# Row maxima and inverse sums of two attention mixers, turned by TensorE or by VectorE

## The chip, the cores and the metric

The kernel runs on one core of a Trainium2 chip. The metric is the device time of one execution in microseconds (us), as the median of several runs. A core has TensorE (PE, matmuls; its weight loads are shown as PEld), VectorE (DVE), ScalarE (ACT), GpSimd (POOL) and SyncE (SP), which here only issues DMAs. Each engine works off its own instructions in order; engines wait for each other at semaphores. SBUF is the working memory with 128 partitions; TensorE writes to PSUM, which has eight banks per partition.

## The reference

One step of a hybrid diffusion layer: 128 context tokens (the prompt) and 1024 latent tokens, width 1024. Each token tile is normalised, modulated and projected to queries, keys, values and gates of two attention mixers, with 8 query heads on 2 key heads each. Mixer A attends over all latent keys and 128 cached ones; mixer B over a band of 128 on each side plus the cached keys, with a learned sink in the softmax:

```python
s = jnp.einsum('bqkgd,bskd->bkgqs', qblk, k_all).astype(jnp.float32) * (d ** -0.5)
p = jax.nn.softmax(s, axis=-1).astype(v_all.dtype)
...
s = jnp.concatenate([sink_column(sink, kv, s_ctx.shape[:-1]), s_ctx, s_band], axis=-1)
p = jax.nn.softmax(s, axis=-1).astype(v_lat.dtype)
...
return jnp.concatenate([o_a * jax.nn.silu(g_a), o_b * jax.nn.silu(g_b)], axis=-1) @ w_out
```

All arrays are float32. The kernel keeps that precision by splitting operands into a high part in fp32r and a low remainder, with two or three products for each.

## The kernel before

The first 280 us hold the modulation, the projections and the gates. The rest is the attention, in units: a unit is one tile of 128 queries (t), one mixer (m = 0 for A, 1 for B) and one group of four heads (g). Units alternate, A then B, so that a pair is one A and one B unit of the same tile and group; there are 16 pairs of latent tiles, and two for the prompt (t = 0). A loop over slots, one slot for one block of 128 keys of one unit, issues all instructions: in each slot first what the agenda holds (`later(n, f)` puts f on it n slots ahead), then the scores of this slot's block, then work that is due there for later units, then products of the output projection, and the value products of the block three slots before. `in_order` at the end keeps each engine's instructions in this order.

**Mixer A.** `max_items` runs ahead of the unit. It takes twelve products `pmx` (L998) of queries and keys, and DVE reduces each to row maxima (L999). `finish` fetches the low part of the queries into the tile qb (L1003, issued by SP) and reduces the twelve maxima of each row to four, one per head, in `m_nat` (L1007): queries lie on the partitions, heads in the columns. The maxima are needed the other way round: as four more rows (64 to 67) of qb, which has queries along its free axis, so that the product of qb with the low keys (L1334) subtracts the maximum as well. `transpose` is put on the agenda by `TURN`. It turns m_nat by a product with the identity into a PSUM bank (`ptm`, L1012), and DVE multiplies the turned rows with `diag`, minus the identity of four, into qb (L1013, one instruction of 4 x 512). The scores `st` (L1333, L1334) then go through ACT's exponential (L1336) and its rounding to the high part (L1340); POOL subtracts for the low part (L1344). `st` lies in the two banks of tag B, so that the scores of one block wait for the exponential two blocks before. Tag A, also two banks, holds `pmx`, `ptm` and part of mixer B's scores.

**Mixer B.** `weight_items` runs ahead of its unit. For each head it makes scores `sn` (L1086, L1087), adds the mask and takes the row maximum on DVE (L1090), and takes the exponential on ACT (L1056) with the row sums. For t > 1 ("boxed") DVE turns the weights in 32 x 32 squares in place (L1066), and DMAs out and back (L1071, L1076) finish the turn. When the unit's slots come, ACT rounds the weights to the high part (L1318) and the low part is subtracted on POOL for even blocks (L1322) and on DVE for odd ones (L1320). The weights aren't divided by their sums; the gate is. `divide` takes the reciprocal of the sums (L1124, again queries on partitions, heads in four columns). `turned` turns it by a product with the identity (`pti`, L1136, tag B for boxed tiles), `put` copies it to SBUF (L1140) and writes it to the DRAM scratch `r_dram` with one DMA (L1141), `rows` fetches it back, spread over 64 partitions for each head (L1146), and POOL multiplies the unit's gate with it (L1132). `ROWS_AT` are their places behind `divide`.

The small tiles m_nat and diag lie in the pool `few`; diag is made on POOL at the start (L372), from the identity.

Of the kernel before, what the change touches and what calls it, by code (L numbers as in the profile page):

```python
# [9 lines left out]
F32 = mybir.dt.float32  # L10
F32R = mybir.dt.float32r
BF16 = mybir.dt.bfloat16
AF = mybir.ActivationFunctionType
ALU = mybir.AluOpType
AX = mybir.AxisListType
# [3 lines left out]
P = 128  # L19
# [20 lines left out]
EARLY = (0, 2)  # L40
# [31 lines left out]
QTS = 5  # L72
PROMPT_LEAD = 4
EX_AT = (2, 2, 5)
ROWS_AT = (1, 1, 4, 6)
BOX_BACK = 2
PROMPT_KEYS_AT = 12
KV_ORDER = [0] + list(range(1, NT))
# [39 lines left out]
def hybrid_step(ctx, tc, x_prompt, x_sample, cache_k_a, cache_v_a, cache_k_b, cache_v_b,  # L118
# [3 lines left out]
    nc = tc.nc  # L122
# [10 lines left out]
    r_dram = [dram.tile([4, P], F32, name=f"rd{i}") for i in range(2 * NL)]  # L133
# [4 lines left out]
    def later(n, f):  # L138

        agenda.setdefault(now[0] + n, []).append(f)  # L140
# [13 lines left out]
    def bank(tag, name):  # L154
        return ps.tile([P, 512], F32, tag=tag, name=name, bufs=BANKS[tag])
# [11 lines left out]
    ident_r = cst.tile([P, P], F32R, name="ident_r")  # L167
# [3 lines left out]
    few = ctx.enter_context(tc.tile_pool(name="few", bufs=1, side="right"))  # L171
# [2 lines left out]
    mhalf = few.tile([P, 8], F32, name="mhalf")  # L174
    nc.vector.memset(mhalf, -0.5)

    m_nat = [few.tile([P, 4], F32R, name=f"m_nat{i}") for i in range(2)]
    diag = few.tile([4, 4], F32, name="diag")
    few.tile([P, 8], F32, name="pad0")

    def rsqrt_mean(pool, ss, n, width, name):

# [150 lines left out]
    with tc.tile_pool(name="st", bufs=2, side="right") as st:  # L333
        ident = st.tile([P, P], F32, name="ident", bufs=1)
# [32 lines left out]
        def conditions():  # L367

            nc.scalar.copy(colt, pcol)
            nc.gpsimd.tensor_scalar(bsc1, colt[:, 32:40], 1.0, None, op0=ALU.add)  # L370
            nc.gpsimd.tensor_copy(ident_r, ident)
            nc.gpsimd.tensor_scalar(diag, ident[0:4, 0:4], -1.0, None, op0=ALU.mult)  # L372

        def modulate_rows(j, half=2):
            if half != 1:
# [136 lines left out]
        for t in (1, 2, 3, 4):  # L512
            squares(t)
            if t == 2:
                nc.scalar.activation(silc, pcol[:, 0:16], AF.Silu)
        conditions()
        for t in (5, 6):
            padded(t, nc.gpsimd)
# [34 lines left out]
        for j in range(1, KT + 3):  # L553
# [68 lines left out]
            if KT - 2 <= j < KT:  # L622
# [3 lines left out]
                c0, n = W_QA.cols[0]  # L626
# [51 lines left out]
    with tc.tile_pool(name="qt", bufs=2, side="right") as qt:  # L678
# [85 lines left out]
        for m in range(2):  # L764
            w, nxt = ((W_QA, W_QB), (W_QB, W_KV))[m]
            ts = list(range(1, NT)) + [0]
            for t in ts:
# [3 lines left out]
                if (m, t) in ((0, ts[-2]), (1, ts[GATE_AT[0]])):  # L771
                    n = len(wg) // 2
# [95 lines left out]
    with ktp:  # L868
# [74 lines left out]
        for n, t in enumerate(KV_ORDER):  # L943
            if n < AHEAD:
                tick()
                pk, v = pks[n]
# [21 lines left out]
    qtile, qbtile, mxtile, sgl = {}, {}, {}, {}  # L968
# [12 lines left out]
    def max_items(i):  # L981

        t, m, g = units[i]
        out = []

        def item(h, b):
            if h == 0 and b == 0:
                mxtile[i] = qs.tile([P, 4, 3], F32, tag="mx", name=f"mx{i}", bufs=3)
            mx = mxtile[i]
            lhs = qtile[i][:, P * h : P * h + P]  # L990
            pm = bank("B" if i == APART + 1 else "A", f"pmx{i}_{h}_{b}")
            if t == 0:
                for h in range(4):
                    hs = slice(P * h, P * h + P)
                    nc.tensor.matmul(pm[:, hs], qtile[i][:, hs], khb[:, g, 0, :], start=True, stop=True)
                nc.vector.tensor_reduce(mx[:, :, 0], pm.rearrange("p (h n) -> p h n", h=4), axis=AX.X, op=ALU.max)
            else:
                nc.tensor.matmul(pm[:, 0:384], lhs, kha[:, g, 3 * b : 3 * b + 3, :], start=True, stop=True)  # L998
                nc.vector.tensor_reduce(mx[:, h, b : b + 1], pm[:, 0:384], axis=AX.X, op=ALU.max)  # L999

        def finish():
            qb_ = qp.tile([68, 512], F32R, tag="qb", name=f"qb{i}", bufs=2)
            nc.sync.dma_start(qb_[0:64, :].bitcast(F32), q_dram[t][m][0:64, 512 * g : 512 * g + 512])  # L1003
            qbtile[i] = qb_
            mx = mxtile.pop(i)
            mn = m_nat[i // 2 % 2]
            nc.vector.tensor_reduce(mn, mx if t else mx[:, :, 0:1], axis=AX.X, op=ALU.max)  # L1007
            later(TURN[boxed(t)], transpose)

        def transpose():  # L1010
            pt = bank("E" if i in EARLY else "A", f"ptm{i}")
            nc.tensor.transpose(pt[0:4, 0:P].bitcast(F32R), m_nat[i // 2 % 2], ident_r)  # L1012
            nc.vector.tensor_tensor(qbtile[i][64:68, :].rearrange("p (h n) -> p h n", h=4),  # L1013
                                    pt[0:4, 0:P].unsqueeze(1).to_broadcast([4, 4, P]),
                                    diag.unsqueeze(2).to_broadcast([4, 4, P]), op=ALU.mult)

        for h in range(4 if t else 1):
            for b in range(3 if t > 0 else 1):
                out.append(lambda h=h, b=b: item(h, b))
        return out, finish  # L1020

    def boxed(t):

        return t > 1
# [5 lines left out]
    def weight_items(i):  # L1030

        t, m, g = units[i]
        v = {}
# [73 lines left out]
        def finish():  # L1107
            (nc.gpsimd if t else nc.vector).tensor_tensor(v["ex"], v["nm"], sink[:, 4 * g : 4 * g + 4], op=ALU.add)
            if t:
                for n, f in zip(EX_AT if i > 3 else EX_EARLY, (sinks, total, divide)):  # L1110
                    later(n, f)
            else:
                sinks()
                later(1, total)
                later(1, divide)
# [5 lines left out]
            (nc.gpsimd if t else nc.vector).tensor_tensor(v["sum"], v["sum"], v["ex"], op=ALU.add)  # L1121

        def divide():
            nc.vector.reciprocal(v["inv"], v["sum"])  # L1124
            if t == 0:
                nc.vector.tensor_tensor(penat[i], penat[i], v["inv"].unsqueeze(2).to_broadcast([P, 4, P]), op=ALU.mult)
                return

            later(ROWS_AT[0], turned)
            later(ROWS_AT[1], put)  # L1130
            later(ROWS_AT[2], rows)
            later(ROWS_AT[3], lambda: nc.gpsimd.tensor_tensor(sgl[i], sgl[i], v["rows"], op=ALU.mult))  # L1132

        def turned():
            v["pt"] = bank("B" if boxed(t) else "A", f"pti{i}")[0:4, 0:P]
            nc.tensor.transpose(v["pt"], v["inv"], ident_r.bitcast(F32))  # L1136

        def put():
            iv = spare[0:4, 512 : 512 + P]
            (nc.vector.tensor_copy if i < 2 or boxed(t) else nc.scalar.copy)(iv, v["pt"])  # L1140
            nc.sync.dma_start(r_dram[i // 2], iv)  # L1141

        def rows():
            v["rows"] = spare[:, 512:768].rearrange("p (c n) -> p c n", c=2)
# [83 lines left out]
    for f in beside[2]:  # L1228
# [5 lines left out]
        name=nc.get_next_instruction_name(), engine=mybir.EngineType.Activation, act_func_set_id=6))  # L1234
# [5 lines left out]
    spare, gate = None, []  # L1240
# [232 lines left out]
    for i, (t, m, g) in enumerate(units):  # L1473
        if i in EARLY:
            continue
        if m == 0:
            items, done = max_items(i)
            at = [start[i - 2] + a for a in (MX_EARLY if i == 4 else MX_AT)]
            end = start[i] - MX_LEAD
            if t == 0:  # L1480
                end = start[i] - LEAD - g
                at = [end - 1]
        else:
            items, done = weight_items(i)
            at = [start[i - 1] + j for j in (NAT_AT if i > 3 else NAT_EARLY)] if t else [start[i] - PROMPT_LEAD]
            end = at[-1] + 1
        if i >= LOADED:
            first = max(start[i - QTS + 1] - 1, at[0] - LOADLEAD[m], 0)
            assert first < at[0] or first == 0, (i, first, at)
            put(first, lambda i=i: u_load(i))  # L1490
        for s, f in zip(at, items):
            put(s, f)
        put(end, done)
# [103 lines left out]
```

## Time and profile before

| what | time |
|---|---|
| median of 3 runs | 682.07 us (681.73 to 682.82) |
| the profiled execution | 683.28 us |
| span of its trace | 681.3 us |
| granted TensorE clock in the span | 0.999 |
| attention, from 300 to 660 us: PE busy | 356.77 of 360 us |
| DVE busy there | 279.35 us |
| ACT busy there | 291.74 us |
| POOL busy there | 271.20 us |

The profile is that of one execution. Its page gives the busy time of each engine, the chain of work that ended last, and the groups of instructions by line: engine, operation, tiles out<-in with their shapes, count, busy time, mean duration in ns, and the idle time of the engine just before them with what ended it. A timeline lists instructions by start time with their duration; "x2" merges neighbours of one group, and brackets tell how long the engine idled before and for what. Matmuls are pipelined: the next one starts before the end shown for the last.

### The profile page before, as it was taken

What the parts mean: (1) busy time and instruction counts of PE and PEld (TensorE: products, weight loads), DVE (VectorE), ACT (ScalarE), POOL (GpSimd) and SP (SyncE); (2) the same over time, 40 slices, a digit from 0 to 9 for tenths busy, and PEclk for the clock granted to TensorE, in tenths of its full rate; (3) what the DMA queues carried; (4) which work ended last, traced back from release to release, by engine and by line L of the source; (5) the groups of instructions that cost most, each with busy time, mean ns of one, the idle gap of its engine ahead of it and who ended that gap; (6) DMA issues with size and microseconds to landing.
All of it is one profiled execution on the core that took longest, in us unless ns stands there. A gap on an engine that the chain in (4) does not pass through costs nothing.

```text
span 681.3 us, 10630 instructions
## 1 busy us (share of the span) xinstructions
PE 671.4 (99%) x3325; PEld 535.6 (79%) x3325; DVE 491.9 (72%) x1055; ACT 403.8 (59%) x834; POOL 373.4 (55%) x378
## 2 busy tenths in 40 slices
PE   8999999999999999999999999999999999999997
PEld 4678988878788888997767777877777777777766
DVE  4776257877787872856788888788787887886663
ACT  6666412411233243169778877877798779878770
POOL 3556024233222250248687669766876787678861
PEclk9999999999999999999999999999999999999999
DMA  8971283349445024541275445664555455544524
GB/s 350 405 266 64 79 314 78 82 91 298 117 117 150 16 90 150 178 140 60 86 201 177 146 151 173 186 191 134 170 178 165 147 161 170 194 124 155 180 68 124
DMA packets 75852, 107.74 MB, mean 158 GB/s; under 512 B 9297, under 2 KB 43533, under 8 KB 75797
## 3 DMA queue, kind: packets, MB, share of 16 engines
q1 hardware_dynamic: 67556, 95.11, 43.6%
q10 hardware_dynamic: 8240, 11.96, 6.5%
q8 instruction: 26, 0.43, 0.2%
q14 instruction: 30, 0.24, 0.1%
HBM read 73.24 MB, written 33.80 MB: 157 GB/s over the span
## 4 chain that ended last, share of the span: by engine, by line
PE 92%; DVE 2%; ACT 2%; DMA 2%; issue 1%; POOL 0%; SPq 0%; ACTq 0%; DVEq 0%
PE po L1434 13%; PE pv L1357 6%; PE pv L1354 6%; PE pmx L998 5%; PE pq L270 5%; PE pq L268 5%; PE pq L269 5%; PE st L1334 5%; PE st L1333 5%; PE pv L1356 5%; PE pg L282 3%; PE pg L278 3%; PE pg L283 3%; PE pk L269 2%; PE pk L270 2%; PE pk L268 2%
## 5 line engine op out<-in xcount | busy, mean ns | idle before, releaser
L1344 POOL TENSOR_TENSOR pl<-pe,ph 128x512 fp32r<-128x512 f32 x128 | 165.8, 1301 | 71.8 <-ACT ph L1340 49.7
L999 DVE TENSOR_REDUCE mx<-pmx 128x1 f32<-128x384 f32 x192 | 100.1, 547 | 28.9 <-PE pmx L998 28.6
L1336 ACT ACTIVATE pe<-st 128x512 f32<-128x512 f32 x146 | 86.6, 593 | 13.3 <-PE st L1334 12.4
L1340 ACT CAST ph<-pe 128x512 fp32r<-128x512 f32 x146 | 90.7, 621 | 5.6
L1354 PE MATMUL pv<-ph,v_hi 128*128 128x512 f32 x208 | 82.2, 395 | 0.2 <-ACT pen L1056 0.2
L1357 PE MATMUL pv<-pl,v_hi 128*128 128x512 f32 x208 | 82.2, 395 | 0.2 <-DVE pl L1330 0.2
L186 POOL TENSOR_TENSOR rs_q<-ms_q,mhalf 128x8 f32<-128x8 f32 x18 | 34.2, 1899 | 80.8 <-DVE ms_q L184 80.8
L1434 PE MATMUL po<-wo,ogh 128*128 128x512 f32 (+1 forms) x224 | 73.3, 387 | 0.0
L1056 ACT ACTIVATE pen<-sn,nm 128x512 f32<-128x512 f32 (+2 forms) x72 | 45.0, 626 | 37.0 <-DVE nm L1090 33.5
L1090 DVE CUSTOM_DVE_ANT_0 sn<-sn,mask,nsink 128x512 f32<-128x512 f32 (+1 forms) x64 | 45.9, 717 | 19.4 <-PE sn L1087 12.5
L998 PE MATMUL pmx<-kha,qt 128*128 128x384 f32 x192 | 58.5, 351 | 0.8 <-DVE mx L999 0.7
L1334 PE MATMUL st<-qb,kla 68*128 68x512 f32 x144 | 57.5, 399 | 0.7 <-DVE qb L1013 0.4
L1333 PE MATMUL st<-qt,kha 128*128 128x512 f32 x144 | 57.8, 401 | 0.0
L1356 PE MATMUL pv<-ph,v_lo 128*64 128x512 f32 x146 | 57.7, 395 | 0.0
L1357 PEld LDWEIGHTS pv<-pl,v_hi 128*128 128x128 f32 x208 | 39.1, 188 | 17.5 <-DVE pl L1330 0.6
L998 PEld LDWEIGHTS pmx<-kha,qt 128*128 128x128 f32 x192 | 36.3, 189 | 13.9 <-DVE mx L999 3.6
L1354 PEld LDWEIGHTS pv<-ph,v_hi 128*128 128x128 f32 x208 | 39.1, 188 | 8.5 <-ACT pen L1056 0.6
L1434 PEld LDWEIGHTS po<-wo,ogh 128*128 128x128 f32 x224 | 41.0, 188 | 5.7 <-ACT ogh L1396 0.3
L747 ACT CAST qo0q<-ptq 128x512 fp32r<-128x512 f32 x18 | 10.6, 587 | 57.8 <-PE ptq L744 57.8
L1434 PE MATMUL po<-wo,ogl 128*128 128x512 f32 (+1 forms) x112 | 43.5, 388 | 0.0
L1322 POOL TENSOR_TENSOR pl<-pen,ph 128x512 fp32r<-128x512 f32 x28 | 37.2, 1328 | 8.1 <-ACT ph L1318 8.1
L1066 DVE STREAM_TRANSPOSE pen<-pen 128x512 f32<-128x512 f32 (+1 forms) x56 | 37.0, 677 | 5.6 <-ACT pen L1056 5.4
(258 smaller groups left out, 1720.5 us busy)
## 6 DMA issues: line engine op xcount, KB each, us to landing
td<-pen SPq DMA_DIRECT2D x24, 512.0 KB
pen<-td SPq DMA_DIRECT2D x96, 128.0 KB
qt<-qd SPq DMA_DIRECT2D x36, 256.0 KB
wm<-in_w_mod_ss_dram SPq DMA_DIRECT2D x7, 1024.0 KB
qd<-qo0q ACTq DMA_DIRECT2D x36, 128.0 KB
qd<-qo1q ACTq DMA_DIRECT2D x36, 128.0 KB
sgl<-gd SPq DMA_DIRECT2D x35, 128.0 KB
out_dram<-yt SPq DMA_DIRECT2D x17, 256.0 KB
```

The costliest lines, as they stand in the source:

```text
L268: nc.tensor.matmul(out, h_at(0, i, k, tok), w.hi[k], start=(k == 0), stop=False)
L998: nc.tensor.matmul(pm[:, 0:384], lhs, kha[:, g, 3 * b : 3 * b + 3, :], start=True, stop=True)
L999: nc.vector.tensor_reduce(mx[:, h, b : b + 1], pm[:, 0:384], axis=AX.X, op=ALU.max)
L1333: nc.tensor.matmul(s, kh, qtile[i], start=True, stop=False)
L1334: nc.tensor.matmul(s, kl, qbtile[i], start=False, stop=True)
L1336: nc.scalar.activation(pe, s, AF.Exp)
L1340: nc.scalar.copy(ph, pe)
L1344: nc.gpsimd.tensor_tensor(pl, pe, ph, op=ALU.subtract)
L1354: nc.tensor.matmul(pv, two, ph, start=(b == 0), stop=False)
L1356: nc.tensor.matmul(pv[0:64, :], vl, ph, start=False, stop=False)
L1357: nc.tensor.matmul(pv, two, pl, start=False, stop=last)
L1434: nc.tensor.matmul(po[n, q.start], a, wo_parts[KT * n + k][lo][:, q], start=(k == KS[0] and p == 0), stop=(k == KS[-1] and p == 2))
```

## The change

m_nat becomes 32 columns wide. Where PE turned it, DVE now turns it in place, in four squares of 32 x 32: the maxima of queries a to a+31 then lie on partitions a to a+3, for a = 0, 32, 64 and 96. Four DVE products of 4 x 128 with a diag that is repeated at those partitions write qb's four rows, 32 queries at a time. In mixer B the reciprocal goes straight into the first four columns of a new tile, `turned_inv`, which DVE turns the same way in the same slot; `put` has no copy left, and writes four DMAs of 4 x 32 numbers in place of one. PE's products `ptm` and `pti` and their banks go. The three tiles are filled with zeros by POOL at the start. The entries of `ROWS_AT` that stay keep their places.

```diff
-ROWS_AT = (1, 1, 4, 6)
+ROWS_AT = (1, 4, 6)
...
-    m_nat = [few.tile([P, 4], F32R, name=f"m_nat{i}") for i in range(2)]
-    diag = few.tile([4, 4], F32, name="diag")
-    few.tile([P, 8], F32, name="pad0")
+    m_nat = [few.tile([P, 32], F32R, name=f"m_nat{i}") for i in range(2)]
+    turned_inv = few.tile([P, 32], F32, name="turned_inv")
+    diag = few.tile([P, 4], F32, name="diag")
+    for a in m_nat + [turned_inv]:
+        nc.gpsimd.memset(a.bitcast(F32), 0.0)
...
-            nc.gpsimd.tensor_scalar(diag, ident[0:4, 0:4], -1.0, None, op0=ALU.mult)
+            for a in range(0, P, 32):
+                nc.gpsimd.tensor_scalar(diag[a : a + 4], ident[a : a + 4, a : a + 4], -1.0, None, op0=ALU.mult)
...
-            nc.vector.tensor_reduce(mn, mx if t else mx[:, :, 0:1], axis=AX.X, op=ALU.max)
+            nc.vector.tensor_reduce(mn[:, 0:4], mx if t else mx[:, :, 0:1], axis=AX.X, op=ALU.max)
             later(TURN[boxed(t)], transpose)
...
         def transpose():
-            pt = bank("E" if i in EARLY else "A", f"ptm{i}")
-            nc.tensor.transpose(pt[0:4, 0:P].bitcast(F32R), m_nat[i // 2 % 2], ident_r)
-            nc.vector.tensor_tensor(qbtile[i][64:68, :].rearrange("p (h n) -> p h n", h=4),
-                                    pt[0:4, 0:P].unsqueeze(1).to_broadcast([4, 4, P]),
-                                    diag.unsqueeze(2).to_broadcast([4, 4, P]), op=ALU.mult)
+            mn = m_nat[i // 2 % 2].bitcast(F32)
+            nc.vector.transpose(mn, mn)
+            for a in range(0, P, 32):
+                nc.vector.tensor_tensor(qbtile[i][64:68, :].rearrange("p (h n) -> p h n", h=4)[:, :, a : a + 32],
+                                        mn[a : a + 4].unsqueeze(1).to_broadcast([4, 4, 32]),
+                                        diag[a : a + 4].unsqueeze(2).to_broadcast([4, 4, 32]), op=ALU.mult)
...
-            nc.vector.reciprocal(v["inv"], v["sum"])
+            nc.vector.reciprocal(turned_inv[:, 0:4] if t else v["inv"], v["sum"])
...
-            later(ROWS_AT[0], turned)
-            later(ROWS_AT[1], put)
-            later(ROWS_AT[2], rows)
-            later(ROWS_AT[3], lambda: nc.gpsimd.tensor_tensor(sgl[i], sgl[i], v["rows"], op=ALU.mult))
-
-        def turned():
-            v["pt"] = bank("B" if boxed(t) else "A", f"pti{i}")[0:4, 0:P]
-            nc.tensor.transpose(v["pt"], v["inv"], ident_r.bitcast(F32))
+            nc.vector.transpose(turned_inv, turned_inv)
+            later(ROWS_AT[0], put)
+            later(ROWS_AT[1], rows)
+            later(ROWS_AT[2], lambda: nc.gpsimd.tensor_tensor(sgl[i], sgl[i], v["rows"], op=ALU.mult))
...
         def put():
-            iv = spare[0:4, 512 : 512 + P]
-            (nc.vector.tensor_copy if i < 2 or boxed(t) else nc.scalar.copy)(iv, v["pt"])
-            nc.sync.dma_start(r_dram[i // 2], iv)
+            for a in range(0, P, 32):
+                nc.sync.dma_start(r_dram[i // 2][:, a : a + 32], turned_inv[a : a + 4])
```

## The prediction

> **What bounds the kernel now.** I read the page first: busy time by engine, then the chain that ended last.
>
> ```profile
> PE 671.4 (99%) x3325; PEld 535.6 (79%) x3325; DVE 491.9 (72%) x1055; ACT 403.8 (59%) x834; POOL 373.4 (55%) x378
> ...
> PE 92%; DVE 2%; ACT 2%; DMA 2%; issue 1%; POOL 0%; SPq 0%; ACTq 0%; DVEq 0%
> ```
>
> TensorE is busy 99% of the span and holds 92% of the chain, so work taken off it looks like time won. But matmul ends are modelled and overlap, so a busy PE can hide short stalls. I therefore went on to the groups by line with shapes kept apart, for what goes and what resembles what comes:
>
> ```profile
> L999 DVE TENSOR_REDUCE mx<-pmx 128x1 f32<-128x384 f32 x192 | 100.1, 547 | 28.9 <-PE pmx L998 28.6
> ...
> L1066 DVE STREAM_TRANSPOSE pen<-pen 128x512 f32<-128x512 f32 x48 | 32.5, 695 | 4.4 <-ACT pen L1056 4.3
> ...
> L1382 DVE TENSOR_TENSOR spare<-pv,rs 64x256 f32<-64x256 f32 x64 | 26.4, 413 | 0.5
> ...
> L1136 PE MATMUL pti<-ident_r,inv 128*4 128x128 f32 x16 | 4.4, 273 | 0.0
> ...
> L1013 DVE TENSOR_TENSOR qb<-ptm,diag 4x512 fp32r<-4x512 f32 x18 | 12.3, 682 | 0.6
> ...
> L1140 DVE COPY spare<-pti 4x128 f32<-4x128 f32 x15 | 4.1, 273 | 0.0
> L1012 PE MATMUL ptm<-ident_r,m_nat 128*4 128x128 f32 x18 | 4.0, 222 | 0.0
> ...
> L1124 DVE RECIPROCAL inv<-sum 128x4 f32<-128x4 f32 x18 | 3.0, 169 | 0.1
> ```
>
> Then the timeline of the attention, one pair of units at a time (some 22.4 us each). First, what one small product really costs PE, by starts:
>
> ```profile
> 354.12 0.40 PE L1357 MATMUL pv<-pl,v_hi 128*128 128x512 f32 x1
> ...
> 354.35 0.22 PE L1012 MATMUL ptm<-ident_r,m_nat 128*4 128x128 f32 x1
> ...
> 354.42 0.44 PE L1086 MATMUL sn<-khb,qt 128*128 128x512 f32 x1
> ...
> 354.70 0.40 PE L1087 MATMUL sn<-klb,qt 128*128 128x512 f32 x1
> ```
>
> A 512-column product hands over after 0.23 us. ptm hands over after 0.07, and the product behind it takes 0.28 instead of 0.23: ptm costs PE 0.12 us, not its 222 ns. I take pti alike. All 34 are worth 34 x 0.12 = 4.1 us if PE never waits.
>
> Second, what PE waits for at the start of a mixer A unit. This is the pair around 402 us:
>
> ```profile
> 400.68 1.30 POOL L1322 TENSOR_TENSOR pl<-pen,ph 128x512 fp32r<-128x512 f32 x1
> ...
> 400.70 1.82 DVE L1320 TENSOR_TENSOR pl<-pen,ph 128x512 fp32r<-128x512 f32 x1
> ...
> 402.24 1.44 POOL L1322 TENSOR_TENSOR pl<-pen,ph 128x512 fp32r<-128x512 f32 x1 [0.26 <-ACT ph L1318]
> ...
> 402.55 0.68 DVE L1013 TENSOR_TENSOR qb<-ptm,diag 4x512 fp32r<-4x512 f32 x1
> ...
> 403.16 0.74 DVE L1090 CUSTOM_DVE_ANT_0 sn<-sn,mask,nsink 128x512 f32<-128x512 f32 x1
> ...
> 404.04 0.69 ACT L1056 ACTIVATE pen<-sn,nm 128x512 f32<-128x512 f32 x1 [1.88 <-DVE nm L1090]
> ...
> 406.50 0.60 ACT L1336 ACTIVATE pe<-st 128x512 f32<-128x512 f32 x1
> ...
> 407.16 0.49 PE L1333 MATMUL st<-qt,kha 128*128 128x512 f32 x1
> ```
>
> This is a chain through DVE and ACT that ends on PE. DVE makes qb (402.55 to 403.23), then adds the mask and takes the row maximum (L1090). ACT has stood idle 1.88 us for that; it runs L1056 and three more instructions without a gap, then L1336, which ends at 407.10 and so frees the bank into which PE writes its next scores at 407.16. **In this pair PE has no slack behind qb: qb later by x is PE later by x.** Around 380 us there is some:
>
> ```profile
> 379.91 1.29 POOL L1322 TENSOR_TENSOR pl<-pen,ph 128x512 fp32r<-128x512 f32 x1 [0.53 <-ACT ph L1318]
> 379.96 0.68 DVE L1013 TENSOR_TENSOR qb<-ptm,diag 4x512 fp32r<-4x512 f32 x1
> ...
> 383.39 0.69 DVE L1320 TENSOR_TENSOR pl<-pen,ph 128x512 fp32r<-128x512 f32 x1 [0.30 <-ACT ph L1318]
> ...
> 383.92 0.60 ACT L1336 ACTIVATE pe<-st 128x512 f32<-128x512 f32 x1
> ...
> 384.99 0.39 PE L1333 MATMUL st<-qt,kha 128*128 128x512 f32 x1
> ```
>
> Here L1336 ends at 384.52 and PE comes at 384.99; less 0.06 for the hand-over, 0.41 us is slack. The same order stands before twelve mixer A units, alternating between these two kinds; the first and the last of the twelve (in the first, the score product L1334 itself waits for qb):
>
> ```profile
> 357.50 0.68 DVE L1013 TENSOR_TENSOR qb<-ptm,diag 4x512 fp32r<-4x512 f32 x1
> ...
> 604.52 0.68 DVE L1013 TENSOR_TENSOR qb<-ptm,diag 4x512 fp32r<-4x512 f32 x1
> ```
>
> Third, the two L1320 above: the same instruction takes 0.69 us alone and 1.82 beside POOL's L1322. It ends 0.54 after POOL does (401.98 to 402.52). L1320 reads both inputs from SBUF. L1013, with one input in PSUM, runs through L1322 in 682 ns every time. So a DVE instruction with two SBUF inputs waits until POOL's subtraction ends. Size doesn't matter:
>
> ```profile
> 644.73 1.28 POOL L1322 TENSOR_TENSOR pl<-pen,ph 128x512 fp32r<-128x512 f32 x1
> ...
> 645.03 1.00 DVE L1103 SCALAR_TENSOR_TENSOR nm<-mx,nsink 128x4 f32<-128x4 f32 x1
> ...
> 652.86 0.16 DVE L1103 SCALAR_TENSOR_TENSOR nm<-mx,nsink 128x4 f32<-128x4 f32 x1
> ```
>
> Four columns take 1.00 us under L1322 and 0.16 without.
>
> **The change, part by part.**
>
> *Removed from PE:* 18 ptm and 16 pti, 0.12 us each. Twelve of each lie in the twelve pairs, between the POOL work that starts the chain and the scores at its end. There PE comes no sooner to the end, so these 24 win nothing. The other ten win 10 x 0.12 = 1.2 us.
>
> *Mixer A on DVE:* qb was one product of 512 columns from PSUM. It becomes a turn of 128x32 and four products of 128 columns, and m_nat and diag now both lie in SBUF. No turn of that size is in the trace: it lies between 169 ns (L1124, four columns) and 695 (L1066, sixteen times as wide); I take 0.2, near the first. It reads one tile and L1066 shows no long cases, so it isn't blocked. The products are:
>
> ```profile
> L664 DVE TENSOR_TENSOR rb_k<-knk,ksin x16: 279/285/486, 207.5 to 252.0; 128x128 f32<-128x128 f32 x16
> ```
> ```profile
> 362.67 0.84 DVE L1382 TENSOR_TENSOR spare<-pv,rs 64x256 f32<-64x256 f32 x2
> ...
> 375.37 0.99 DVE L999 TENSOR_REDUCE mx<-pmx 128x1 f32<-128x384 f32 x2
> ```
>
> One takes 0.285. Two L999 (547 ns each, above) take 0.99 together, so neighbours overlap by some 0.08 to 0.1; the two halves of L1382 (413 each), on other partitions, take 0.84, so they don't overlap. The new products read other partitions each time: 0.30 apart; the other end is 0.20.
>
> Now the order in time. L1320 ends, the turn runs 0.2 us, and meanwhile POOL's next L1322, whose input is there, has begun. The first product waits for its end. By L1320's rows 0.15 of an instruction's own time passes under the wait (0.69 less 0.54), so 0.14 of the 0.285 is left. Then come three more, 0.90. At 402: 403.68 + 1.04 = 404.72 instead of 403.23, **1.49 later**. At 380: 381.20 + 1.04 = 382.24 instead of 380.64, 1.60 later, 1.19 after the slack. L1090 stands behind qb on DVE, L1056 waits for it, PE for L1336, as above. With seven of the first kind and five of the second: 7 x 1.49 + 5 x 1.19 = **16.4 us**. If PE came late only where ACT does, and everything else moves with it, nothing gives it back: PE is the bound for the rest of the pair.
>
> By the Trainium skill, "VectorE: DVE Perf Modes", section "Two Vector instructions with no wait between them", an instruction whose input starts in another group of 32 partitions than the last one's is held until all earlier ones end. The four products would each be held, which fits L1382's row; without it the spacing would be 0.20 and the sum 12 x 0.3 = 3.6 us less.
>
> *Mixer B on DVE:* the turn (0.2) comes in right behind the reciprocal, and the copy (0.27), a little later, goes. Around 375 us the L999 shown last stands directly behind the reciprocal, and PE waits for it:
>
> ```profile
> 375.95 0.44 PE L998 MATMUL pmx<-kha,qt 128*128 128x384 f32 x1
> ```
>
> There L998 comes 0.2 later, but this is PE time ahead of the chain's end, which hides it. Uncovered it costs 5 x 0.2 = 1.0. ptm and pti also give up their places in banks A and B; the bank wait that ends on PE is the one for L1336, and that stays.
>
> *SP:* 48 more issues, 0.26 us each.
>
> ```profile
> 395.74 0.38 SPq L1305 DMA_DIRECT2D sgl<-gd  x1
> 398.87 0.26 SPq L1141 DMA_DIRECT2D rd<-spare  x1
> 399.18 0.47 SPq L1003 DMA_DIRECT2D qb<-qd  x1
> ```
>
> The queue is idle before L1141 and the turned sums are there sooner than the copy was, so the four mostly fit in. Queued behind them is the fetch for qb, issued at 399.18 and needed by the scores after 403; late by all of 3 x 0.26 = 0.78 it would still have 3 us. I take nothing; without that cover it is at most 12 x 0.78 = 9 us. *Start:* three fills and three more scalings of diag on POOL, which then idles 4.16 us; nothing:
>
> ```profile
> 15.59 1.30 POOL L468 TENSOR_TENSOR h<-hf,h 128x512 fp32r<-128x512 f32 x1 [4.16 <-DVE hf L467]
> ```
>
> Sum: 683.28 (the profiled execution) + 16.4 - 1.2 = 698.5. The median shown is 682.07, 1.2 lower: **697.3**.
>
> **The rivals.**
>
> *PE time counts, faster.* For it: the 99%. Place: the 24 products in the pairs; it decides if the first product gets its read before POOL's second L1322, or if ACT makes up the lateness before PE needs the bank. Price: -34 x 0.12 = -4.1, 678.0. Against: ACT's idle 1.88 us ahead of L1056, and no gap after it. By the Trainium skill, same page, section "Rules for kernel authors", VectorE is the fastest for a turn within 32x32; no run here shows that for this size. Chance 0.10.
>
> *No wait for POOL, the products apart as L1382's.* qb is then 0.2 - 0.08 + 0.90 + 0.285 = 1.3 after L1320, against 0.71 before: 0.6 later. 7 x 0.6 + 5 x 0.2 - 1.2 = +4, 686. For it: the new tiles have four partitions, and no blocked instruction in the trace has so few. Chance 0.20.
>
> *No wait and overlapping products.* 0.3 later, 7 x 0.3 - 1.2 = +0.9, 683.0, about no change. L664's last products speak for it, L1382 against. Chance 0.07.
>
> **How the numbers follow.** The forecast, 0.63: 690 (spacing 0.20, some lateness made up) to 703 (no slack in the second kind, 5 x 0.41 = 2.0, the turn's 1.0, and some 2 for the prompt's two units, where POOL is busy too). With the second rival the range is 685 to 703; left out are the rivals that aren't slower, 0.17. A difference of 0.2% (1.4 us) is about the least that a measurement of this kernel tells from none. Faster 0.10, same 0.07, slower 0.83.
>
> **What would show it.** Right: the first of the four qb products ends some 0.14 us after an L1322, lasting near 1 us, three follow 0.3 apart; ACT's idle time ahead of L1056 grows from 1.88 to over 3; PE waits on L1336 in every pair; POOL is unchanged. Wrong: products of 0.3 us while L1322 runs, or PE's gaps before L1333 no longer than now.

## The result and the profile after

The changed kernel takes 707.85 us (median of 4 executions, 706.47 to 709.1) where the kernel before took 681.91 beside it: 1.038 times as long, with an interval of 1.036 to 1.040. It is 25.9 us slower; forecast were 15.2 (697.3), and 703 was the end of the range. The direction was right and the size was not.

One line from the page of the kernel before, then the page of the kernel after: busy time by engine, the chain that ended last, and groups by line (busy time, mean ns, idle time before them and what ended it). Line numbers differ between the kernels: L1334 of before is L1333 of after.

```profile
L1334 PE MATMUL st<-qb,kla 68*128 68x512 f32 x144 | 57.5, 399 | 0.7 <-DVE qb L1013 0.4
```
```profile
PE 679.8 (96%) x3291; PEld 533.9 (75%) x3291; DVE 520.0 (74%) x1128; ACT 403.0 (57%) x833; POOL 375.9 (53%) x384
...
PE 69%; DVE 17%; DMA 4%; ACT 4%; issue 3%; POOL 1%; SPq 1%; ACTq 0%; DVEq 0%; POOLq 0%
...
L1333 PE MATMUL st<-qb,kla 68*128 68x512 f32 x144 | 58.7, 407 | 11.0 <-DVE qb L1017 11.0
...
L1017 DVE TENSOR_TENSOR qb<-m_nat,diag 4x128 fp32r<-4x128 f32 x72 | 42.7, 593 | 1.4
```

PE's share of the chain falls from 92% to 69% and DVE's rises from 2% to 17%. The score product with qb, which waited 0.7 us before, now waits 11 us for it. The mean of 593 ns for the new products hides two kinds; the view of one line shows them (shortest, median, longest; first and last start), and so does the group of the two turns:

```profile
L1017 DVE TENSOR_TENSOR qb<-m_nat,diag x72: 282/286/1411, 282.4 to 677.9; 4x128 fp32r<-4x128 f32 x72
```
```profile
L1015 DVE STREAM_TRANSPOSE m_nat<-m_nat 128x32 f32<-128x32 f32 x18 | 3.6, 201 | 0.0
L1133 DVE STREAM_TRANSPOSE turned_inv<-turned_inv 128x32 f32<-128x32 f32 x16 | 3.4, 212 | 0.5
```

Half of the products take 0.286 us or less, as forecast, and some take four to five times that. The turn takes 0.20, as forecast. This is the timeline at the pair which the prediction showed around 402 us, now around 407:

```profile
406.71 0.69 DVE L1319 TENSOR_TENSOR pl<-pen,ph 128x512 fp32r<-128x512 f32 x1
406.77 3.08 POOL L1321 TENSOR_TENSOR pl<-pen,ph 128x512 fp32r<-128x512 f32 x2
407.32 0.20 DVE L1015 STREAM_TRANSPOSE m_nat<-m_nat 128x32 f32<-128x32 f32 x1
...
407.55 3.04 DVE L1017 TENSOR_TENSOR qb<-m_nat,diag 4x128 fp32r<-4x128 f32 x4
...
409.42 0.39 PE L1332 MATMUL st<-qt,kha 128*128 128x512 f32 x1
...
410.62 0.76 DVE L1094 CUSTOM_DVE_ANT_0 sn<-sn,mask,nsink 128x512 f32<-128x512 f32 x1
...
410.65 0.50 PE L1333 MATMUL st<-qb,kla 68*128 68x512 f32 x1 [0.84 <-DVE qb L1017]
...
411.52 0.69 ACT L1060 ACTIVATE pen<-sn,nm 128x512 f32<-128x512 f32 x1 [3.35 <-DVE nm L1094]
```

DVE's subtraction L1319 now starts 0.06 us ahead of POOL's L1321. It gets through in 0.69, and POOL's is the one that is stretched: two of them take 3.08 back to back, where 2 x 1.3 would be their own time. The four products run into both of POOL's instructions: the first one waits for one, and before the second product starts POOL has begun the next. All four take 3.04 us, where the run with POOL's fill, below, shows 1.18. And PE stands at L1333, the product that reads qb, 1.23 us after the start of L1332 instead of 0.23 (403.50 to 403.73 before, shown below).

### The profile page after: what moved, and what is told of

Same layout as the page of the kernel before. It is cut to its first block, busy times and chain, and to the rows that moved or that the text cites. A ratio compares the mean times of both kernels' runs of the same rounds, so it can differ in the third digit from the quotient of the medians.

```text
span 707.4 us, 10649 instructions
## 1 busy us (share of the span) xinstructions
PE 679.8 (96%) x3291; PEld 533.9 (75%) x3291; DVE 520.0 (74%) x1128; ACT 403.0 (57%) x833; POOL 375.9 (53%) x384
## 4 chain that ended last, share of the span: by engine, by line
PE 69%; DVE 17%; DMA 4%; ACT 4%; issue 3%; POOL 1%; SPq 1%; ACTq 0%; DVEq 0%; POOLq 0%
PE po L1433 9%; DVE qb L1017 5%; PE st L1332 4%; PE pq L270 4%; PE pq L272 4%; PE pq L271 4%; PE st L1333 4%; PE pv L1353 3%; PE pmx L1001 3%; PE pv L1356 3%; PE pg L280 3%; PE pg L284 3%; PE pg L285 3%; PE pv L1355 2%; PE pk L271 2%
## 5 line engine op out<-in xcount | busy, mean ns | idle before, releaser
L1333 PE MATMUL st<-qb,kla 68*128 68x512 f32 x144 | 58.7, 407 | 11.0 <-DVE qb L1017 11.0
L1332 PE MATMUL st<-qt,kha 128*128 128x512 f32 x144 | 60.1, 417 | 2.0 <-DVE pl L1329 0.6
L1321 POOL TENSOR_TENSOR pl<-pen,ph 128x512 fp32r<-128x512 f32 x28 | 38.9, 1395 | 11.7 <-ACT ph L1317 10.2
L1017 DVE TENSOR_TENSOR qb<-m_nat,diag 4x128 fp32r<-4x128 f32 x72 | 42.7, 593 | 1.4
```

Of the source, the lines that this page charges most:

```text
L1332: nc.tensor.matmul(s, kh, qtile[i], start=True, stop=False)
L1333: nc.tensor.matmul(s, kl, qbtile[i], start=False, stop=True)
```

## The experiments

Theory 1: the loss is the products' wait for POOL's reads of SBUF, since both their inputs now lie there. Theory 2: it is the DVE work itself, a turn and three more products on the way to qb. Theory 3: it is mixer B's half, its turn and its four small DMAs. Times are medians; the kernel before took 682.1 to 682.3 beside all of these.

### Each half alone

Mixer A's half alone: the kernel after with

```diff
-ROWS_AT = (1, 4, 6)
+ROWS_AT = (1, 1, 4, 6)
...
-            nc.vector.transpose(turned_inv, turned_inv)
-            later(ROWS_AT[0], put)
+            later(ROWS_AT[0], turned)
+            later(ROWS_AT[1], put)
...
```

> Mixer A's half of the change alone: DVE turns the maxima and multiplies them from SBUF, mixer B's inverse is turned by PE and copied as before. Theory 1 (the loss is qb's products, which have both inputs in SBUF and wait for POOL's reads, handed on over DVE, ACT and the bank to PE): 705 to 709 us, and the first or second of the four products near 1.1 to 1.3 us in every pair. Theory 3 (mixer B's turn and its 48 more DMAs cost it): 682 to 688 us.

Measured: 707.05 us (706.38 to 707.51).

Mixer B's half alone: the kernel before, with turned_inv, its turn and its four DMAs.

> Mixer B's half of the change alone. Theory 1: 679 to 682 us, since sixteen small products of PE go, at 0.12 us each by starts, of which only those beside no wait win. Theory 3 (mixer B's turn and its DMAs cost the 26 us): 700 us or more.

Measured: 679.56 us (679.07 to 680.98), 0.997 of before, interval 0.996 to 0.998: within what theory 1 gave, and faster than both kernels.

The whole loss is mixer A's, and theory 3 falls. The 2.6 us that mixer B's half wins alone (1.3 to 2.9 by the interval) are about what the rival "PE time counts" gives for its sixteen small products, 16 x 0.12 = 1.9. In the kernel after nothing is left of them: it takes 707.0 to 707.9 with that half and 707.05 without. Where PE waits for qb in every pair, earlier PE time buys nothing.

### The same DVE work without the wait

In the kernel before, qb from four products out of PSUM, and a turn of a tile of zeros on DVE:

```diff
+            nc.vector.transpose(turned_m, turned_m)
+            for a in range(0, P, 32):
+                nc.vector.tensor_tensor(qbtile[i][64:68, :].rearrange("p (h n) -> p h n", h=4)[:, :, a : a + 32],
+                                        pt[0:4, a : a + 32].unsqueeze(1).to_broadcast([4, 4, 32]),
+                                        diag.unsqueeze(2).to_broadcast([4, 4, 32]), op=ALU.mult)
```

> The kernel before, where PE still turns the maxima, but qb comes from four products of 4x128 that read the turned maxima in PSUM, and DVE also turns a tile of zeros: all the DVE work of mixer A's half and one small product of PE more than after, but no product with two inputs in SBUF. Theory 1: the work alone moves qb later by the turn of 0.20 us and three more products at 0.2 to 0.3, near 1.0 us, of which the pairs without slack hand on most: 682 to 692 us, products 0.25 to 0.3 us long. Theory 2 (it is the DVE work itself that costs, not the wait for POOL): 700 us or more.

Measured: 681.09 us (680.48 to 682.93), 0.999 of before, interval 0.998 to 1.000. The expectation had the four products too slow: they take 0.2 us more than the one product of 0.68, since they follow 0.20 apart. 700 us, as theory 2 had it, are far off. But the run doesn't show that this work is free. From one reduction of m_nat to the next, the pairs like that at 380 us go from 22.15 to 22.44 us, and those like that at 402 us from 22.73 to 22.40. In the latter DVE's subtraction (L1323 here) now gets ahead of POOL's and takes 0.69 us, as in the kernel after, where the kernel before has up to 1.82.

```profile
399.38 3.10 POOL L1325 TENSOR_TENSOR pl<-pen,ph 128x512 fp32r<-128x512 f32 x2
399.39 0.69 DVE L1323 TENSOR_TENSOR pl<-pen,ph 128x512 fp32r<-128x512 f32 x1
```

The kernel after with the turned maxima in PSUM:

```diff
-            nc.vector.transpose(mn, mn)
+            pt = bank("E" if i in EARLY else "A", f"ptm{i}")[:, 0:32]
+            nc.vector.transpose(pt, mn)
...
-                                        mn[a : a + 4].unsqueeze(1).to_broadcast([4, 4, 32]),
+                                        pt[a : a + 4].unsqueeze(1).to_broadcast([4, 4, 32]),
```

> The kernel after, but the turned maxima are written to a PSUM bank, so that the four products have one input in SBUF and one in PSUM; the small products of PE are gone as in the kernel after. Theory 1: no product waits for POOL any more and each lasts 0.3 us: qb comes about 0.6 us later than before, which gives 680 to 690 us. Theory 2: as the kernel after, 700 us or more.

Measured: 684.94 us (684.67 to 686.32), 1.005 of before, interval 1.003 to 1.007. The products of the run with PE's turn come first, in the view of their line and, for one unit, in the timeline; then those of this run in the same two views:

```profile
L1016 DVE TENSOR_TENSOR qb<-ptm,diag x72: 271/272/283, 282.2 to 649.9; 4x128 fp32r<-4x128 f32 x72
```
```profile
400.21 0.88 DVE L1016 TENSOR_TENSOR qb<-ptm,diag 4x128 fp32r<-4x128 f32 x4
```
```profile
L1018 DVE TENSOR_TENSOR qb<-ptm,diag x72: 281/288/296, 282.5 to 653.4; 4x128 fp32r<-4x128 f32 x72
```
```profile
401.68 3.03 POOL L1322 TENSOR_TENSOR pl<-pen,ph 128x512 fp32r<-128x512 f32 x2
...
402.49 1.19 DVE L1018 TENSOR_TENSOR qb<-ptm,diag 4x128 fp32r<-4x128 f32 x4
```

With one input in PSUM none of the 72 products is long in either run, POOL's subtractions notwithstanding: in the last fence the four start 0.8 us into POOL's two, and take 1.19. The one placement of the turned maxima is worth 22 us (707.01, below, to 684.94). Theory 2 is left with the rest: 684.94 is 5.4 us above mixer B's half alone, for a turn in the way of qb and products 0.30 apart.

The timelines also part the spacings: four products that all start at partition 0 take 0.88 us, (0.88 - 0.27) / 3 = 0.20 apart; four that start at partitions 0, 32, 64 and 96 take 1.19, 0.30 apart. By the Trainium skill, "VectorE: DVE Perf Modes", section "Two Vector instructions with no wait between them", only the latter are held until the one before has ended; these runs agree.

### POOL writes but doesn't read

POOL's subtraction for mixer B's even blocks becomes a fill, in the kernel before and in the kernel after:

```diff
-                nc.gpsimd.tensor_tensor(pl4, p, ph4, op=ALU.subtract)
+                nc.gpsimd.memset(pl.bitcast(F32), 0.0)
```

> The kernel before, in which POOL fills the low part of the even blocks of mixer B's weights with zeros instead of subtracting (the low part of those blocks is left out of the result). POOL then writes but reads nothing in SBUF there. It is the base for the next run. Both theories: 679 to 683 us, since POOL is not the bound.

Measured: 678.50 us (677.89 to 678.83). It fell 3.6 us under before, a little below what both theories gave. Here DVE's subtraction of the odd blocks, which also reads two tiles of SBUF, never waits: all 26 take 0.65 to 0.69 us, also where one starts 0.29 us behind the start of POOL's fills. In the kernel before, such a place took 1.57 us (378.36).

```profile
376.59 0.99 POOL L1322 MEMSET pl<- 128x512 f32 x2
376.88 0.69 DVE L1320 TENSOR_TENSOR pl<-pen,ph 128x512 fp32r<-128x512 f32 x1
```

> The kernel after with the same fill on POOL (the low part of those blocks is left out of the result). Theory 1 (qb's products wait because POOL reads SBUF at that time): the products beside the fill last 0.29 us again, and the distance to the run with the fill in the kernel before falls from 26 to 3 to 8 us, with what the prompt's units lose to POOL's other subtractions on top of the 3 us that the turn into PSUM cost. Theory 2 (any work of POOL holds them): the distance stays at 20 us or more.

Measured: 681.94 us (681.75 to 684.14), 3.4 us above the run with the fill in the kernel before. By the reductions of m_nat in the two traces, none of that lies in the twelve pairs (266.5 us before, 266.4 after): 1.4 lie ahead of them and 2.2 behind, where POOL's other subtractions still run. The timeline of one unit:

```profile
400.77 0.69 DVE L1319 TENSOR_TENSOR pl<-pen,ph 128x512 fp32r<-128x512 f32 x1
400.81 0.99 POOL L1321 MEMSET pl<- 128x512 f32 x2
...
401.37 0.20 DVE L1015 STREAM_TRANSPOSE m_nat<-m_nat 128x32 f32<-128x32 f32 x1
...
401.61 1.18 DVE L1017 TENSOR_TENSOR qb<-m_nat,diag 4x128 fp32r<-4x128 f32 x4
```

The four products take 1.18 together, 0.30 apart, although all inputs are in SBUF. The fill is also shorter than the subtraction (0.53 us against 1.3), and the first product starts only 0.19 us before the fills end, so these rows alone don't part reads from busy time. The subtraction that runs through the fills in 0.69 does. By the Trainium skill, "SBUF — State Buffer", section "Who interferes with whom", a VectorE instruction with two SBUF inputs contends with a GpSimd instruction that reads SBUF and not with one that only writes; this run agrees.

### The prompt's two units, and the turn moved up

In the kernel after, PE's turn and the one product again for t = 0 only:

```diff
+            if t == 0:
+                pt = bank("A", f"ptm{i}")
+                nc.tensor.transpose(pt[0:4, 0:P].bitcast(F32R), m_prompt[g], ident_r)
...
+                return
```

> The kernel after, but in the prompt's two units PE turns mixer A's maxima and one product makes qb from PSUM, as before. Theory 1, with the waits under POOL in the prompt costing the last 4.5 us of the difference: 703 to 705 us. If the prompt's late products lie beside other work: 707 to 708 us.

Measured: 702.52 us (702.06 to 703.61), 4.5 below the 707.01 of the kernel after in its second run. The prompt's units are a term of their own. In the kernel after they look like this, one of the two; the last rows are PE's there and behind it:

```profile
664.22 3.84 POOL L1343 TENSOR_TENSOR pl<-pe,ph 128x512 fp32r<-128x512 f32 x3
...
665.92 4.31 DVE L1017 TENSOR_TENSOR qb<-m_nat,diag 4x128 fp32r<-4x128 f32 x4
...
668.02 0.79 POOL L1398 TENSOR_TENSOR ogl<-spare,ogh 128x256 fp32r<-128x256 f32 x1
...
668.76 1.32 POOL L1321 TENSOR_TENSOR pl<-pen,ph 128x512 fp32r<-128x512 f32 x1
...
670.28 0.50 PE L1333 MATMUL st<-qb,klb 68*128 68x512 f32 x1 [0.77 <-DVE qb L1017]
...
675.70 0.63 PE L1327 MATMUL st<-ident_r,pen 128*128 128x128 f32 x4 [2.58 <-DVE m_nat L1015]
```

Each of the four products waits for another of POOL's instructions, 4.31 us in all, and PE stands 0.77 and 2.58 us for what DVE does late; of the 2.58 the kernel before has 1.09 at the same place. In the run with PE's turn the one product takes 0.68 there.

Now the turn straight behind the reduction, products where they were, in the kernel after and in the one with the turn into PSUM:

```diff
+            nc.vector.transpose(mn.bitcast(F32), mn.bitcast(F32))
             later(TURN[boxed(t)], transpose)
...
-            nc.vector.transpose(mn, mn)
```

> The kernel after, with the turn of the maxima issued straight behind the reduction that makes them, some 3 us earlier, where VectorE stands idle 0.6 us; the four products stay where they were. If the turn's 0.2 us lies on the chain of each of the twelve pairs: 2.4 us less, 704 to 706 us. If POOL's subtraction sets the first product's end whatever stands ahead of it: 706.5 to 708 us.

Measured: 706.75 us (706.05 to 707.53). The turn isn't on the path: DVE comes to the products sooner and waits longer, until POOL ends.

> The turn written to PSUM, and moved up in the same way. No product waits for POOL, so what stands ahead of the first product counts. Turn on the chain: 12 x 0.2 = 2.4 us less than 684.94 where there is no slack, 682 to 684 us; what is then left against 679.56 (mixer B's half alone) is the 0.30 us spacing of the four products. If the turn was hidden: 684.5 to 685.5 us, unless the bank, held longer, makes PE wait, which would give more.

Measured: 683.75 us (682.76 to 685.69), 1.0026 of before, interval 1.001 to 1.004. It is 1.2 us less than 684.94, half of what was expected of a turn on the chain of every pair, though the two runs' times overlap. From one reduction to the next, the median pair of the kind at 380 us goes from 22.63 to 22.48 us and that of the kind at 402 us from 22.56 to 22.52: here the second kind has slack. What remains against mixer B's half alone is 4.2 us.

Mixer B's half with four products from PSUM was tried as a still faster version:

> Mixer B's half of the change alone, with PE's turn of the maxima as before, and qb from four products of 4x128 out of PSUM. A candidate for the fastest: mixer B's half alone gave 679.56 us and the four products from PSUM 681.09 (against 682.16). If the two gains add: 678.5 us. If the second was the measurement's spread: 679.0 to 680.5.

Measured: 680.11 us (679.44 to 682.19), 0.997 of before, interval 0.996 to 0.998. The gains don't add: beside mixer B's half the four products win nothing. That half alone remains the fastest of the kernels that leave nothing out.

### The kernel after once more

> The kernel after once more, for the number of its executions: two of the four so far had a mean granted clock of 0.995 and took 709.0 and 709.1 us, two had 0.998 and 1.0 and took 706.5 and 706.7. If the cut of the clock is what parts them, executions at 0.998 or more fall near 706.6 and those near 0.995 some 2.4 us higher; if not, times and clock go apart.

Measured: 707.01 us (706.22 to 708.23). All eight executions of this kernel, by PE's mean granted clock (1.0 is full speed): 706.26, 706.7 at 1.0; 706.22, 706.47 at 0.998; 707.76 at 0.997; 708.23, 708.99, 709.1 at 0.995. Those below 0.998 are 1.1 to 2.9 us longer than those at 0.998 or more. In the run of mixer A's half alone time and clock don't go together in this way (707.21 us at 1.0, 706.88 at 0.997). The first profiled execution is the one of 709.1. Here are ACT's and PE's rows at its first pair, from the timeline, and from the windows view two stretches of 3.4 us (busy time and instructions of PE, PEld, DVE, ACT and POOL, granted clock, DMA share, GB/s); then this run's rows and its second stretch:

```profile
356.81 1.14 ACT L1317 CAST ph<-pen 128x512 fp32r<-128x512 f32 x2 [3.12 <-DMA qb<-qd]
...
361.57 0.50 PE L1333 MATMUL st<-qb,kla 68*128 68x512 f32 x1 [1.99 <-DVE qb L1017]
```
```profile
359.60:363.00 3.40, 1.43 (x6) 1.04 (x6) 3.30 (x8) 0.55 (x1) 0.88 (x1) 1.00 0.04 10
...
363.00:366.40 3.40, 3.29 (x8) 2.48 (x8) 3.11 (x7) 3.27 (x8) 0.11 (x1) 0.51 0.44 154
```
```profile
355.01 1.14 ACT L1317 CAST ph<-pen 128x512 fp32r<-128x512 f32 x2 [1.73 <-DMA rd<-turned_inv]
...
360.05 0.50 PE L1333 MATMUL st<-qb,kla 68*128 68x512 f32 x1 [1.07 <-DVE qb L1017]
```
```profile
363.00:366.40 3.40, 3.40 (x15) 2.37 (x13) 3.37 (x9) 3.26 (x7) 1.62 (x2) 1.00 0.67 231
```

In the first execution data for ACT arrived some 1.8 us later (which DMA it was, the profile infers). PE's wait for qb grew from 1.07 to 1.99 us, and the clock was then halved for 3.4 us: 8 matmuls instead of 15. Why the data was late in that execution isn't settled. All this makes that pair 27.53 us long, from one reduction to the next, instead of 24.64, which is the 2.9 us between the two spans (707.4 and 704.5). That the other long executions lost their time in the same way is not shown. Some 24 us are lost without it.

## Why the prediction was off

The sum of the runs, from 682.16: mixer B's half -2.6 (679.56); mixer A's work with one input in PSUM +5.4 (684.94); the wait for POOL +22.1 (707.01). Giving the prompt's two units back to PE takes 4.5 off the whole.

Where the time lies in the span, by the reduction of m_nat ahead of the first of the twelve pairs and the one behind the last: the rows of before, then those of the second run of the kernel after (its span is 704.5 us, that of before 681.3).

```profile
353.18 0.14 DVE L1007 TENSOR_REDUCE m_nat<-mx 128x4 fp32r<-128x12 f32 x1
...
622.84 0.14 DVE L1007 TENSOR_REDUCE m_nat<-mx 128x4 fp32r<-128x12 f32 x1
```
```profile
354.41 0.16 DVE L1010 TENSOR_REDUCE m_nat<-mx 128x4 fp32r<-128x12 f32 x1
...
641.64 0.17 DVE L1010 TENSOR_REDUCE m_nat<-mx 128x4 fp32r<-128x12 f32 x1
```

| stretch | forecast | measured |
|---|---|---|
| up to the first pair, and behind the twelfth | -1.2 (ten small products of PE) | +1.2 and +4.4 |
| the twelve pairs | +16.4 | (641.64 - 354.41) - (622.84 - 353.18) = +17.6 |
| sum | +15.2 | +23.2 (704.5 - 681.3) |

The medians are further apart, by 24.7 (707.01 and 682.34), since the profiled execution of before was longer than its median and that of after shorter.

**The step that failed is the count of units: "The other ten win 10 x 0.12 = 1.2 us", and a sum over twelve pairs only.** The price of the wait was worked out for the twelve pairs and applied to them alone; the six other mixer A units were entered with PE's gain and no wait. Their share is 6.8 of the 8.0 us by which the spans differ from the forecast. The prediction knew that POOL is busy in the prompt and named some 2 us for it, but only in the range. In the runs each of POOL's instructions there catches another product (4.31 us for four). The last unit ahead of the prompt waits too: its four take 2.80 in the second run. Up to the first pair one product is caught (the longest, 1411 ns in the first execution); it makes some 0.7 of that 1.2, since the run with the turn into PSUM has its second reduction at 294.35 where the kernel after has 295.05. The rest isn't settled.

**The wait, right.** Products with two SBUF inputs wait for POOL's subtraction however few elements they have; the second rival's doubt about four partitions fell. Its price without the wait, +4 and 686, came near the 684.94 measured with the turn into PSUM (+2.8), but by luck. Its sum had 0.6 us for each pair like that at 402 us, and 0.2 for each like that at 380. Measured, from one reduction to the next, the former go from 22.73 to 22.56, since DVE's subtraction now gets ahead of POOL's, and the latter from 22.15 to 22.63. So the kind of pair that was to have slack is the one that pays.

**The sum per pair, 1.37 forecast and 1.46 measured, is near for partly wrong reasons.** Forecast was that the first product waits once, with L1320 held by POOL before as ever. In the changed kernel DVE's subtraction goes first in five of the twelve pairs (second run), and gains what it lost before (1.82 to 0.69), and POOL comes in between the products: in one kind of pair the first two wait, in the other the second. The kind at 380 us loses 1.45 and that at 402 us 1.67 from one reduction to the next, where 1.19 and 1.49 were forecast, so the slack of 0.41 bought less than assumed.

**The path, wrong in its last part.** The prediction took qb's lateness through L1090 and L1056 on to L1336 and the bank. ACT's idle time did grow from 1.88 to 3.35. But PE doesn't come that far: it stands at L1333, which reads qb itself, 0.84 us in the pair shown, twelve times in the twelve pairs of the second run (9.3 us in all), and the bank adds little: the next L1332 starts 0.27 us late (412.36). The prediction had that only for the first pair. In the pair at 402 us qb ended 0.5 us before its first reader in the kernel before (403.23, and L1334 at 403.73). It now ends 3.88 us after the start of DVE's subtraction (406.71 to 410.59) instead of 2.53 (400.70 to 403.23), and 1.35 goes past that 0.5.

```profile
403.50 0.40 PE L1333 MATMUL st<-qt,kha 128*128 128x512 f32 x1
...
403.73 0.40 PE L1334 MATMUL st<-qb,kla 68*128 68x512 f32 x1
```

**The small products in the pairs "win nothing": right here, not in general.** With qb late it held (707.0 with or without mixer B's half). With qb on time mixer B's half, with the same sixteen products gone, wins 2.6 us. In the pairs behind the first it is 0.07 us for each of one kind (22.73 to 22.66) and 0.13 for the other (22.15 to 22.02), near the 0.12 of a small product; the first pair is 1.1 shorter, which isn't explained.

**Mixer B's turn and the DMAs.** The turn isn't quite hidden: in the run of that half alone PE waits for the reductions behind it eight times where it did twice before (the waits view of either, us in total, times, longest).

```profile
PE pmx L999 <- DVE mx L1000: 3.2, 8, 0.7
```
```profile
PE pmx L998 <- DVE mx L999: 0.7, 2, 0.4
```

That half gains all the same. Its 48 more issues on SP cost nothing that these runs show. Right were also the turn's 0.20, the spacing of 0.30 and POOL's busy time, 375.9 us after 373.4.

## What to carry to other kernels

When an operand moves from PSUM to SBUF, look up on the timeline what POOL reads at that moment, for every place where the instruction is issued and not only in the steady loop: writing the turned tile to PSUM instead was worth 22 us here. Several short DVE instructions in a row can each wait for another POOL instruction, so split work costs one wait for each piece, not one in all. A small saving on the busiest engine counts only where that engine isn't made to wait for the same change's other half.

## What the hardware showed that was not expected

POOL's instructions come in between DVE's back-to-back products: four products of 0.28 us took 3.04 us in a pair and 4.31 in the prompt, with a new wait of up to 1.1 (1411 ns less 286) for a POOL instruction. The order of start can decide who waits: L1319 took 0.69 where it started 0.06 us ahead of POOL's L1321, and 1.82 (as L1320) where it started 0.02 behind. So close together the start shown doesn't settle it: in the run with four products out of PSUM, DVE's took 0.69 although it started 0.01 behind (399.39).

Behind a PE stall of 2 us the granted clock was halved for 3.4 us; behind one of 1.07 us in the same place it was not. That the stall is the cause was not tried by itself. By the Trainium skill, "TensorE: Matmul & The Clock Gate", section "What's actually happening", the clock is decided in windows of 3413 ns by whether PE is busy, with the half rate after an idle window; the length agrees, while here PE was busy for 1.43 of the 3.40 us ahead of the half rate.
